# Linear attention staged one level ahead, operand splits shared with GpSimd at the half turn, and final rows reordered in a hybrid mixer and ConvFFN layer

## The chip, the cores and the metric

The kernel runs on one core of a Trainium2 chip. The metric is the device time of one execution in microseconds (us). Three runs of the kernel before gave 2209.49, 2205.0 and 2207.99 us, median 2207.99. The trace comes from one further execution of 2208.4 us, whose profiled span is 2206.6 us. Below, times in a trace count from the start of that span.

## What is computed

One decoder layer on x of 2048 positions by 1024 channels, all float32:

```
h = rms_norm(x, norm_mix_pre);  p = h @ w_in          # u, v_a, q, k, v_b, g_out, lr
out_a = u * (tril(w_s) @ layer_norm(v_a) + b_s)       # chunks of 128, 4 heads, after gelu
gk = log_sigmoid(lr @ w_gk + b_gk) / 16
out_b = rms_norm(gla(q, k, v_b, gk)) * silu(g_out)    # gated linear attention, 4 heads
x = x + rms_norm(concat(out_a, out_b) @ w_out, norm_mix_post)
up = causal_dwconv(rms_norm(x, norm_ffn_pre) @ w_up)  # 3 taps, 2 x 2816 channels
ff = (gelu(up[:, :2816]) * up[:, 2816:]) @ w_down
x = x + rms_norm(ff, norm_ffn_post)
```

## The kernel before

Every large product is made from float32r operands. An operand is split into a high part, which ScalarE casts (`A.copy(out=hi, in_=raw)`), and a low part, raw minus high, which `split_lo` (L77) gives to VectorE or to GpSimd. Three TensorE products, high by high, high by low and low by high, accumulate in PSUM, so nothing can be multiplied before both engines have split it.

The work has three phases. **Mixing** goes through four batches of 512 positions (`mix_in`). A batch makes q and k, then weaves two generators: `main`, which runs the gated linear attention of its two halves (`gla_half`), and `side`, which makes the other projections (`token_steps`: one weight chunk and its 24 products between two yields) and the output projection of the batch before (`mix_out`, tiles mx0a and mx1a). `weave` adds a ratio for each step of `main` and runs one step of `side` whenever the sum reaches one. `gla_half` first makes the decayed keys (kd, transposed to kps) and the diagonal (qk, dps). Then it goes through seven levels of distance s = 64 to 1 (`LEVELS`): VectorE forms two differences of the cumulated gates (e), ScalarE exponentiates, VectorE and GpSimd multiply into qup and klow, TensorE makes the scores (tile lv), and VectorE copies them by a mask into attn. Products with v (tiles o, s), a norm, and a transpose (tile ot, `finish`) follow. Here a scheduler orders each engine's queue by priority, which follows the order in which the code was written.

The last `mix_out` and the first operands of the next phase form the **seam**: seven combinations of the normalised x are loaded from DRAM (tiles ta) and split, and 22 up-projection units start.

**Up** makes both halves of the positions (1024 each) in 22 units of a seven-product fast matrix multiplication (`prod`, L725; products in the order 0, 5, 6, 4, 1, 3, 2, each of 12 matmuls). At the turn from the first half (units u00 to u021) to the second (u10 to u121) all seven operands (tiles tb) are loaded and split anew by `op_split` (L652 to L657). **Down** does the same for w_down in steps of half, product and group (`dsteps`; matmuls on L1077), while `plan` (L1097) hangs the final norm and the store of finished rows on certain steps: `fin_load` fetches x, `fin_scale` squares a row and takes the root, `fin_row` scales, adds x and stores. From the first up unit to the end, `in_order` (L615) fixes each engine's queue to the order of the code. All loads and stores of these phases are issued by SP, one after the other; an issue waits until its tile is free.

The FFN code runs through `op_split(acts[4])`, `op_split(acts[1])`, `op_split(acts[3])` and `op_split(acts[2])` in the first unit of the second half (`new`, from L934), all with the low parts on VectorE.

Of the kernel before, what the change touches and what calls it, by code (L numbers as in the profile page):

```python
# [37 lines left out]
def layer_kernel(ctx, tc, x, xT, w_ch, w_gl, w_tk, w_o, w_up, w_dn, w_gk, wsT, cols, conv, rows, sgub,  # L38
# [73 lines left out]
    def token_steps(srcs, kper, n, hh, hl, name, done):  # L112
        nk = kper * len(srcs)
        ps = [bank(f"{name}a{t}", acc=True) for t in range(TT)]
        for i, src in enumerate(srcs):
# [12 lines left out]
            yield last.ins  # L128

# [14 lines left out]
    def mix_phase(mp, late):  # L144
# [57 lines left out]
        def mix_in(b, prev):  # L202
# [215 lines left out]
        return mix_out(NB - 1, *prev)  # L418

    def gla_half(b, hb, cum, qT, kT, vb, sg, ohb, olb, state, attn, klow, qup, lvl_sb, sel_sb, w1, pend):  # L420
# [16 lines left out]
        kps = bank(f"{n}kps")  # L437
        for c in range(2):
            for ht in range(2):
                o = (c * 2 + ht) * P  # L440
                PE.transpose(out=kps[:, o:o + P], in_=kd[:, ht, c * P:(c + 1) * P], identity=ident)
        kdec = w1.tile([P, 512], F32, tag="kdec", name=f"{n}kdec", bufs=1)
        A.copy(out=kdec, in_=kps)
# [3 lines left out]
        dps = bank(f"{n}dps")  # L447
        for c in range(2):
            for ht in range(2):
                o = c * 4 + ht * 2  # L450
                PE.matmul(dps[:, o:o + 2], lhsT=qk[:, ht, c * P:(c + 1) * P], rhs=sel_sb,
                          start=True, stop=True)
        dg = w1.tile([P, 8], F32, tag="dg", name=f"{n}dg")
        V.tensor_copy(out=dg, in_=dps[:, 0:8])
        yield

        for li, s in enumerate(LEVELS):
            if li == 4 and pend:
                pend.pop()()
                yield  # L460
            g = 256 // (2 * s)
            gc = P // (2 * s)
# [12 lines left out]
            for par in range(2):  # L475
# [6 lines left out]
                            in1=ev[:, :, :, 0, :], op=ALU.mult)  # L482
            mk = lvl_sb[:, li * 64:(li + 1) * 64].rearrange("p (g s) -> p g s", s=s)
            ps = bank(f"{n}lv{s}")
            for c in range(2):
                for ht in range(2):
                    o = (c * 2 + ht) * P
                    PE.matmul(ps[:, o:o + P], lhsT=kl[:, ht, c * P:(c + 1) * P],
                              rhs=qu[:, ht, :, c * 64:(c + 1) * 64], start=True, stop=True)
            av = attn.rearrange("p c h (g two s) -> p (c h) g two s", two=2, s=s)  # L490
            V.copy_predicated(out=av[:, :, :, 1, :], mask=mk.unsqueeze(1).to_broadcast([P, 8, gc, s]),
                              data=ps.rearrange("p (x g s) -> p x g s", x=8, s=s))
# [3 lines left out]
        for c in range(2):  # L496
            t = hb * 2 + c
            ops = bank(f"{n}o{c}")
            for ht in range(2):
                PE.matmul(ops[:, ht * 256:(ht + 1) * 256], lhsT=eb[:, ht, c * P:(c + 1) * P],  # L500
                          rhs=state[:, ht, :], start=True, stop=False)
                for par in range(2):
                    h = ht * 2 + par
                    hs = slice(h * P, (h + 1) * P)
                    PE.matmul(ops[:, hs], lhsT=attn[:, c, h, :], rhs=vb[t][:, hs],
                              start=False, stop=(par == 1))
            sps = bank(f"{n}s{c}")
            for h in range(NH):
                r = slice((h % 2) * 64, (h % 2) * 64 + 64)
                o = c * 256 + h * 64  # L510
                PE.matmul(sps[r, (h // 2) * P:(h // 2 + 1) * P], lhsT=kdec[:, o:o + 64],
# [115 lines left out]
    def ffn_phase(fp, mix_rest, late):  # L627
# [142 lines left out]
        class Side:  # L770
# [3 lines left out]
            def scale(self):  # L774
                pass
# [446 lines left out]
```

## Time and profile before

| | |
|---|---|
| median of three runs | 2207.99 us |
| profiled execution: time, span | 2208.4 us, 2206.6 us |
| TensorE busy | 2102.8 us (95%), 9904 matmuls |
| VectorE, ScalarE, GpSimd busy | 1570.1, 963.7, 710.3 us |
| DRAM traffic | 345.65 MB, 157 GB/s over the span |

Busy time is the union of an engine's instructions. The clock column of the stretches below is the share of TensorE's full 2.4 GHz that was granted: 1.00 is 2.4 GHz, 0.50 is 1.2 GHz. In the wait view, "A <- B: t, n, m" says that A waited for B, t us in all, n times, at most m. In a timeline, the bracket at a row's end is the idle time of the engine before it and what ended it.

### The profile page before, as it was taken

Reading aid. Unit: us, or ns where it says so; the run is one execution under the profiler, and the core shown is the slowest. Engines: PE = TensorE matmul, PEld = TensorE weight load, DVE = VectorE, ACT = ScalarE, POOL = GpSimd, SP = SyncE. Lnnn points to the kernel's source line nnn. Section 1 sums busy time; section 2 is a strip of 40 time slices with the busy share of each in tenths; the row PEclk is TensorE's granted clock in tenths of the full one; section 3 lists DMA queues with packets and bytes.
Section 4 is the critical chain, followed back from the end, with each engine's and each line's share of the span. In section 5 each row is a group of like instructions: output and inputs, shape, how many; then the busy total and the mean of one; then the engine's idle time right before and its main releaser. Section 6 shows DMA issues by size and latency. Waiting matters only on the chain.

```text
span 2206.6 us, 27110 instructions
## 1 busy us (share of the span) xinstructions
PE 2102.8 (95%) x9904; PEld 1737.2 (79%) x9904; DVE 1570.1 (71%) x2039; ACT 963.7 (44%) x1536; POOL 710.3 (32%) x481
## 2 busy tenths in 40 slices
PE   8998999999999889999999997999999999999997
PEld 7787877787788767788888876877787778888876
DVE  6776757666766465788878879999999952344366
ACT  5444435444545545444455544334333333332342
POOL 3322232232312224555545544555555300000000
PEclk9999999999999999999999998999999999999999
DMA  8422245225423626455445463434444544344465
GB/s 280 136 69 72 75 152 169 74 77 169 156 87 103 217 92 221 178 183 183 147 145 185 149 228 110 158 133 163 162 153 157 201 148 151 129 155 154 146 252 224
DMA packets 139366, 338.80 MB, mean 154 GB/s; under 512 B 13008, under 2 KB 42080, under 8 KB 139232
## 3 DMA queue, kind: packets, MB, share of 16 engines
q1 hardware_dynamic: 134336, 328.57, 44.0%
q10 hardware_dynamic: 4896, 8.50, 1.1%
q8 instruction: 78, 1.28, 0.2%
q14 instruction: 56, 0.46, 0.1%
HBM read 245.26 MB, written 100.40 MB: 157 GB/s over the span
## 4 chain that ended last, share of the span: by engine, by line
PE 39%; DVE 18%; issue 4%; DMA 3%; ACT 2%; POOL 1%; SPq 0%; DVEq 0%; POOLq 0%; ACTq 0%
PE d0C L1077 3%; PE d1A L1077 3%; PE d1C L1077 3%; PE d0A L1077 3%; PE d0D L1077 2%; PE d1D L1077 1%; PE d1B L1077 1%; PE d0B L1077 1%; DVE ds L580 1%; DVE dw L579 1%; DVE dw L581 1%; DMA dw<-in_w_dn 1%; DVE ds L578 1%; PE u015G L725 0%; PE u017G L725 0%
## 5 line engine op out<-in xcount | busy, mean ns | idle before, releaser
L1064 POOL TENSOR_TENSOR o010r<-o010r,mhalf 128x4 f32<-128x4 f32 x1 | 1.0, 1007 | 357.1 <-DVE o010r L1063 357.1
L77 DVE TENSOR_TENSOR tal<-tal,tah 128x1024 fp32r<-128x1024 f32 x14 | 24.7, 1811 | 10.8 <-ACT tah L657 10.8
L77 DVE TENSOR_TENSOR tbl<-tbl,tbh 128x1024 fp32r<-128x1024 f32 x14 | 18.7, 1390 | 8.8 <-ACT tbh L657 8.8
L1077 PE MATMUL d0D<-d2wl,d02th 128*128 128x512 f32 x44 | 18.0, 408 | 3.8 <-DVE d2wl L77 3.8
L1077 PE MATMUL d0A<-d0wh,d00th 128*128 128x512 f32 x44 | 18.5, 420 | 2.8 <-DVE u121y L752 2.8
L77 DVE TENSOR_TENSOR d11tl<-d11tl,d11th 128x1024 fp32r<-128x1024 f32 (+1 forms) x6 | 6.6, 1134 | 20.3 <-ACT d11th L657 20.3
L77 DVE TENSOR_TENSOR d05tl<-d05tl,d05th 128x1024 fp32r<-128x1024 f32 (+1 forms) x6 | 6.6, 1133 | 19.7 <-ACT d05th L657 19.7
L1045 DVE TENSOR_TENSOR r<-d0C,du 128x512 f32<-128x512 f32 x8 | 5.2, 686 | 21.7 <-PE d0C L1077 21.7
L77 DVE TENSOR_TENSOR d01tl<-d01tl,d01th 128x1024 fp32r<-128x1024 f32 (+1 forms) x6 | 6.6, 1134 | 18.0 <-ACT d01th L657 18.0
L1077 PE MATMUL d0A<-d0wl,d00th 128*128 128x512 f32 x44 | 18.3, 417 | 0.0
L1077 PE MATMUL d0A<-d0wh,d00tl 128*128 128x512 f32 x44 | 18.1, 412 | 0.0
L77 DVE TENSOR_TENSOR d10tl<-d10tl,d10th 128x1024 fp32r<-128x1024 f32 (+1 forms) x6 | 6.6, 1135 | 16.2 <-ACT d10th L657 16.2
L477 POOL TENSOR_TENSOR qup<-b3q,b3h1e 64x256 f32<-64x256 f32 x7 | 6.0, 855 | 36.9 <-issue 15.0
L581 DVE TENSOR_TENSOR dw<-dw,ds 128x512 f32<-128x512 f32 x11 | 17.4, 1580 | 0.4
L580 DVE TENSOR_TENSOR ds<-dw,dw 128x512 f32<-128x512 f32 x11 | 17.4, 1579 | 0.4
L579 DVE TENSOR_TENSOR dw<-dw 128x512 f32<-128x512 f32 x11 | 17.4, 1578 | 0.4
L1077 PE MATMUL d0D<-d2wh,d02tl 128*128 128x512 f32 x44 | 17.6, 400 | 0.0
L1077 PE MATMUL d0D<-d2wh,d02th 128*128 128x512 f32 x44 | 17.6, 400 | 0.0
L1064 POOL TENSOR_TENSOR o110r<-o110r,mhalf 128x4 f32<-128x4 f32 x1 | 4.3, 4251 | 41.3 <-DVE o110r L1063 41.3
L1077 PE MATMUL d0A<-d1wl,d01th 128*128 128x512 f32 x44 | 17.1, 389 | 0.0
L1077 PE MATMUL d1B<-d5wl,d15th 128*128 128x512 f32 x44 | 17.1, 389 | 0.0
L1077 PE MATMUL d1D<-d2wl,d12th 128*128 128x512 f32 x44 | 17.1, 389 | 0.0
(4592 smaller groups left out, 8460.9 us busy)
## 6 DMA issues: line engine op xcount, KB each, us to landing
dw<-in_w_dn SPq DMA_DIRECT2D x22, 512.0 KB, 5.2
out<-r SPq DMA_DIRECT2D x16, 512.0 KB, 5.7
tal<-act SPq DMA_DIRECT2D x14, 512.0 KB, 6.6
tbl<-act SPq DMA_DIRECT2D x14, 512.0 KB, 6.4
wdn<-in_w_dn SPq DMA_DIRECT2D x6, 1024.0 KB, 7.4
wdn<-dw SPq DMA_DIRECT2D x22, 256.0 KB, 2.3
wdn<-ds SPq DMA_DIRECT2D x22, 256.0 KB, 3.1
d00tl<-ffs SPq DMA_DIRECT2D x5, 512.0 KB, 8.4
```

The lines of the kernel that those rows point to most:

```text
L77: eng.tensor_tensor(out=lo, in0=full, in1=hi.bitcast(F32), op=ALU.subtract)
L477: (G if par else V).tensor_tensor(out=qu[r, :, par, :].rearrange("p a (g s) -> p a g s", s=s), in0=view(q)[r, :, :, 1, :], in1=ev[r, :, :, ...
L578: eng.tensor_tensor(out=t3, in0=b22, in1=b12, op=ALU.subtract)
L579: eng.tensor_tensor(out=b12, in0=b12, in1=b11, op=ALU.subtract)
L580: eng.tensor_tensor(out=t2, in0=b22, in1=b12, op=ALU.subtract)
L581: eng.tensor_tensor(out=t4, in0=b21, in1=t2, op=ALU.subtract)
L1045: return V.tensor_tensor(out=row(half, o[0], t)[:, o[1] * T:(o[1] + 1) * T], in0=ps, in1=u, op=ALU.add)
L1064: G.tensor_tensor(out=rr[:, sl], in0=rr[:, sl], in1=mhalf[:, sl], op=ALU.pow)
L1077: ins = PE.matmul(ps, lhsT=lhs, rhs=wop[w][:, i], start=start and k == 0, stop=stop and k == 2, skip_group_check=more)
```

## The change

Four edits go together.

1. **Attention.** The e, exponent and product work of a level moves into `decays(li)`, which is written one level ahead of the scores of the level before; `scores`, the transposes and the products with v are pinned by `issue_after(newest_pe())` behind the last TensorE instruction written so far. In each chunk the state products (s) come ahead of the output products (o). Two more yields stand ahead of the last `finish` of a batch, and the weaving ratio goes from 0.85 to 0.8.
2. **Seam.** The first step of the last `mix_out` is written while the mixing pools are still open. The first unit's weights are split after the fourth operand of the seam instead of the second (the order of operands is 0, 5, 6, 4, 1, 3).
3. **Turn.** `op_split` takes an engine. Operand 4 is split one unit earlier, with its low parts on GpSimd; operand 3 goes to GpSimd; operand 1 comes behind the copy `copy_u2`.
4. **Final rows.** The x rows of the first finished quarter go into idle low-weight tiles and are all loaded at step last-7. The squares of the first 512 columns of the last four rows are summed two steps before the last (`part_scale`); at the end each row squares only its other 512 columns, the row before is finished while its own scale is made, and the last quarter's rows are scaled, added and stored in two halves.

```diff
+    def newest_pe():
+        return next(i for i in reversed(nc.cur_bb.bb.instructions) if i.engine == ET.PE)
...
                     yield from gla_half(b, hb, cum, qT, kT, vb, sg, ohb, olb, state, attn[hb], klow, qup,
                                         lvl_sb, sel_sb, w1, pend)
+                yield
+                yield
                 pend.pop()()
...
-            weave(main(), side(), (0.85, 0.85) if prev is not None else (0.62, 0.5))
+            weave(main(), side(), (0.8, 0.8) if prev is not None else (0.62, 0.5))
...
-        return mix_out(NB - 1, *prev)
+        rest = mix_out(NB - 1, *prev)
+        next(rest)
+        return rest
...
+        ready = decays(0)
+        yield
+        with tc.issue_after(newest_pe()):
...
+        for li in range(len(LEVELS)):
+            if li == 4 and pend:
+                pend.pop()()
+                yield
+            now = ready
+            if li + 1 < len(LEVELS):
+                ready = decays(li + 1)
+            scores(li, *now)
             yield
...
-        def op_split(op):
+        def op_split(op, eng=V):
...
-                split_lo(V, lo[:, sl], raw[:, sl], hi[:, sl])
+                split_lo(eng, lo[:, sl], raw[:, sl], hi[:, sl])
...
-        next(mix_rest)
...
-            if m == 5:
+            if m == 4:
                 prep = Prep("u00", first, raw4("u00s23"), raw4("u00s14"))
...
-            if new:
-                op_split(acts[4])
             product(0, None if end else pa)
...
-            if new:
-                op_split(acts[1])
...
                 copy_u2 = A.copy(out=f.u2, in_=pa)
+            if new:
+                op_split(acts[1])
             if nxt:
                 nxt.sums()
                 nxt.split(0)
+            if new:
+                op_split(acts[3], G)
...
-            if new:
-                op_split(acts[3])
...
                 op_split(pre[6])
+                op_split(pre[4], G)
...
-        plan = {last - 6: [lambda: loads(0, 1, 0, 1), lambda: scale(0, 1)],
-                last - 5: [lambda: finish(0, 1, 0, 1), lambda: loads(0, 1, 2, 3)],
-                last - 4: [lambda: finish(0, 1, 2, 3), lambda: loads(1, 1, 0, 1, 2, 3)],
+        plan = {last - 7: [lambda: loads(0, 1, 0, 1, 2, 3)],
+                last - 6: [lambda: scale(0, 1)],
+                last - 5: [lambda: finish(0, 1, 0, 1)],
+                last - 4: [lambda: finish(0, 1, 2, 3)],
...
             done = evac(m, half, t)
-            fin_row(half, 0, t, fin_scale(half, 0, [t]))
+            A.activation(out=junk[:, :T], in_=row(1, 0, t)[:, T:], func=AF.Square, accum_out=tail[:, t:t + 1])
+            if t:
+                fin_row(half, 0, t - 1, rt[:, t - 1:t], 2)
+            V.tensor_scalar(out=rt[:, t:t + 1], in0=tail[:, t:t + 1], scalar1=1.0 / D, scalar2=part[:, t:t + 1],
+                            op0=ALU.mult, op1=ALU.add)
+            G.tensor_tensor(out=rt[:, t:t + 1], in0=rt[:, t:t + 1], in1=mhalf[:, :1], op=ALU.pow)
+        fin_row(half, 0, TT - 1, rt[:, TT - 1:TT], 2)
```

The built program's queues show what moved. TensorE's queue at the end of the second half of batch 2, from the last level's scores (lv) to the first output products with attn (o<-b2vb,attn); vaa are projections. Before:

```order
L488 MATMUL b2h1lv_4465<-qup_206,klow_210 128x128 x4
L500 MATMUL b2h1o_4471<-state,b2h1eb 128x256
L123 MATMUL b2vaa_4580<-hb2vaw_4585,b2hi_3260 128x512
L124 MATMUL b2vaa_4580<-lb2vaw_4586,b2hi_3260 128x512
L125 MATMUL b2vaa_4580<-hb2vaw_4585,b2lo_3261 128x512
L123 MATMUL b2vaa_4580<-hb2vaw_4585,b2hi_3264 128x512
L124 MATMUL b2vaa_4580<-lb2vaw_4586,b2hi_3264 128x512
L511 MATMUL b2h1s_4478<-b2vb_3256,b2h1kdec 64x128 x4
```

Now:

```order
L481 MATMUL b2h1lv_4461<-qup_206,klow_210 128x128 x4
L524 MATMUL b2h1s_4468<-b2vb_3256,b2h1kdec 64x128 x4
L527 MATMUL b2h1o_4467<-state,b2h1eb 128x256
L532 MATMUL b2h1o_4467<-b2vb_3256,attn_204 128x128 x2
L527 MATMUL b2h1o_4467<-state,b2h1eb 128x256
L532 MATMUL b2h1o_4467<-b2vb_3256,attn_204 128x128 x2
```

Before, 14 projections lay between the last scores and the first o<-attn (the rows that follow those shown are nine more of them); now none does. Ahead of these scores stand 10 projections instead of 6, and ahead of the batch's last transposes 34 in one piece instead of 28. The place of kps and dps in the first half, 13 projections behind q and k and one more between the two, is the same in both.

SP's queue at the seam, where b3mx0w and b3mx1w are the weight chunks of the last output projection, u0r the raw weights of the first up unit, and tal the operands. Before:

```order
L86 DMA rb3u_6716<-in_w_ch 128x1024
L86 DMA rb3mx0w_6785<-in_w_o 128x1024
L86 DMA rb3mx0w_6831<-in_w_o 128x1024
L662 DMA u0rg<-in_w_up 128x1024
L86 DMA rb3mx0w_6869<-in_w_o 128x1024
L663 DMA u0rv<-in_w_up 128x1024
L86 DMA rb3mx0w_6941<-in_w_o 128x1024
L650 DMA tal_6824<-act_89 128x1024 x2
```

Now:

```order
L86 DMA rb3u_6716<-in_w_ch 128x1024
L86 DMA rb3mx0w_6764<-in_w_o 128x1024
L86 DMA rb3mx0w_6831<-in_w_o 128x1024
L86 DMA rb3mx0w_6869<-in_w_o 128x1024
L684 DMA u0rg<-in_w_up 128x1024
L685 DMA u0rv<-in_w_up 128x1024
L86 DMA rb3mx0w_6907<-in_w_o 128x1024
L86 DMA rb3mx1w_6965<-in_w_o 128x1024
L672 DMA tal_6824<-act_89 128x1024 x2
```

The first chunk (6785, now 6764) takes a tile of the mixing pool, and u0rv no longer stands behind the third chunk.

VectorE's queue at the turn, from the last split of the first half's last unit to the sums of the second half's first unit. Before:

```order
L77 TENSOR_TENSOR tbl_10687<-tbl_10687,tbh_10686 128x1024 x2
L77 TENSOR_TENSOR tbl_10710<-tbl_10710,tbh_10709 128x1024 x2
L897 TENSOR_TENSOR u021G<-u021G,u021u_10635 128x512
L749 SCALAR_TENSOR_TENSOR u021yv<-u021V,cv,u021yv 128x1023
L749 SCALAR_TENSOR_TENSOR u021yv<-u021V,cv,u021yv 128x1022
L77 TENSOR_TENSOR tbl_10731<-tbl_10731,tbh_10730 128x1024 x2
```

Now:

```order
L77 TENSOR_TENSOR tbl_10687<-tbl_10687,tbh_10686 128x1024 x2
L918 TENSOR_TENSOR u021G<-u021G,u021u_10635 128x512
L770 SCALAR_TENSOR_TENSOR u021yv<-u021V,cv,u021yv 128x1023
L770 SCALAR_TENSOR_TENSOR u021yv<-u021V,cv,u021yv 128x1022
L77 TENSOR_TENSOR tbl_10731<-tbl_10731,tbh_10730 128x1024 x2
```

Operand 4's pair (10710) has left VectorE here, and so has operand 3's pair behind the sums; operand 1's (10731) and, further on, operand 2's stay.

## Rows read from the trace of the kernel before

**Rows 1.** The page: TensorE's busy share in the 40 slices.

```profile
PE   8998999999999889999999997999999999999997
```

**Rows 2.** Stretches: mixing, seam, up, down, tail (us, engines' busy us, clock, DMA).

```profile
0.00:819.80 819.80, 769.72 (x4104) 646.87 (x4104) 542.16 (x925) 394.14 (x684) 215.96 (x158) 0.97 0.39 128
819.80:878.10 58.30, 49.25 (x193) 38.91 (x194) 34.97 (x23) 32.67 (x50) 25.26 (x11) 0.91 0.65 226
2193.10:2206.60 13.50, 0.02 (x1) 0.00 (x0) 5.93 (x7) 1.78 (x4) 1.08 (x2) 0.64 0.27 108
```

**Rows 3.** TensorE's waits in mixing.

```profile
PE b2h1ot L546 <- DVE b2h1os L537: 3.2, 2, 2.5
...
PE h2t L605 <- ACT h2x L590: 3.1, 1, 3.1
...
PE b2h1lv L488 <- DVE x1rm L557: 2.6, 1, 2.6
```

**Rows 4.** Stretches of batch 2: the wait for the last level, and what follows.

```profile
531.88:534.46 2.58, 0.00 (x1) 0.03 (x1) 2.55 (x5) 1.01 (x2) 1.60 (x2) 1.00 1.05 361
534.70:538.10 3.40, 3.40 (x13) 3.03 (x13) 2.33 (x3) 0.00 (x0) 1.01 (x1) 0.50 0.86 330
```

**Rows 5.** Timelines of VectorE and GpSimd around that wait.

```profile
530.23 2.63 DVE L477 TENSOR_TENSOR qup<-b2q,b2h1e 64x256 f32<-64x256 f32 x1
...
530.19 2.39 POOL L77 TENSOR_TENSOR lb2vaw<-rb2vaw,hb2vaw 128x1024 fp32r<-128x1024 f32 x1 [6.98 <-ACT hb2vaw L89]
```

**Rows 6.** TensorE's waits at and behind the seam, and two stretches of the seam.

```profile
PE b3mx0a L123 <- ACT hb3mx0w L89: 4.1, 1, 4.1
...
PE b3mx1a L124 <- POOL lb3mx1w L77: 3.1, 1, 3.1
...
PE u00V L725 <- DVE u00u L966: 2.9, 1, 2.9
...
PE b3mx0a L124 <- POOL lb3mx0w L77: 1.7, 1, 1.7
...
824.83:831.65 6.82, 5.36 (x13) 4.20 (x14) 2.63 (x2) 0.62 (x1) 2.76 (x2) 0.50 0.72 262
...
859.20:877.80 18.60, 18.60 (x82) 15.15 (x81) 8.27 (x6) 10.05 (x15) 2.41 (x1) 1.00 0.43 172
```

**Rows 7.** TensorE's waits at the turn and the clock across the longer one.

```profile
PE u10V L725 <- DVE u10u L966: 10.9, 1, 10.9
...
PE u10G L725 <- ACT u10u L944: 3.6, 1, 3.6
...
1333.42:1347.05 13.63, 5.57 (x13) 4.44 (x14) 11.48 (x12) 4.95 (x7) 6.74 (x4) 0.50 0.11 39
```

**Rows 8.** VectorE's and GpSimd's timelines at the turn.

```profile
1315.64 4.63 DVE L77 TENSOR_TENSOR tbl<-tbl,tbh 128x1024 fp32r<-128x1024 f32 x4 [2.21 <-ACT tbh L657]
...
1329.73 3.42 DVE L77 TENSOR_TENSOR tbl<-tbl,tbh 128x1024 fp32r<-128x1024 f32 x2
...
1338.37 2.36 DVE L77 TENSOR_TENSOR tbl<-tbl,tbh 128x1024 fp32r<-128x1024 f32 x2 [2.12 <-ACT tbh L657]
...
1326.55 1.52 POOL L77 TENSOR_TENSOR u11w0l<-u1rg,u11w0h 128x512 fp32r<-128x512 f32 x1 [14.81 <-ACT halo L758]
```

**Rows 9.** The wait in down's product D, VectorE ahead of it, and the clock behind it.

```profile
PE d0D L1077 <- DVE d2wl L77: 3.8, 1, 3.8
...
2133.13 1.22 DVE L1071 TENSOR_TENSOR r<-r,o6x 128x1024 f32<-128x1024 f32 x1 [5.26 <-DMA o6x<-x]
...
2142.37:2145.78 3.41, 3.12 (x7) 2.48 (x8) 3.41 (x6) 2.27 (x4) 1.88 (x1) 0.50 1.02 414
```

**Rows 10.** The tail: last evacuation, square, scaling and addition of the last row.

```profile
2197.09 0.68 DVE L1045 TENSOR_TENSOR r<-d1D,du 128x512 f32<-128x512 f32 x1
2197.87 1.06 ACT L1060 ACTIVATE o103q<-r 128x1024 bf16<-128x1024 f32 x1 [4.14 <-DVE r L1045]
2201.25 1.22 DVE L1071 TENSOR_TENSOR r<-r,o11x 128x1024 f32<-128x1024 f32 x1
```

More of the change, by code (lines that the diff above doesn't have):

```diff
@@ L436, in gla_half, with decays @@
         V.tensor_tensor(out=kd, in0=kd, in1=k, op=ALU.mult)
[L437 to L443, printed above, removed]
         qk = w1.tile([P, 2, 256], F32, tag="lv", name=f"{n}qk", bufs=4)
         V.tensor_tensor(out=qk, in0=q, in1=k, op=ALU.mult)
[L447 to L460, printed above, removed]
+        def decays(li):
+            s = LEVELS[li]
             g = 256 // (2 * s)
-            gc = P // (2 * s)
             def view(ap):
@@ L487, in gla_half @@
                     o = (c * 2 + ht) * P
[L488 to L492, printed above, removed]
+                    PE.transpose(out=kps[:, o:o + P], in_=kd[:, ht, c * P:(c + 1) * P], identity=ident)
+            for c in range(2):
+                for ht in range(2):
+                    o = c * 4 + ht * 2
+                    PE.matmul(dps[:, o:o + 2], lhsT=qk[:, ht, c * P:(c + 1) * P], rhs=sel_sb,
+                              start=True, stop=True)
+        kdec = w1.tile([P, 512], F32, tag="kdec", name=f"{n}kdec", bufs=1)
+        A.copy(out=kdec, in_=kps)
+        dg = w1.tile([P, 8], F32, tag="dg", name=f"{n}dg")
+        V.tensor_copy(out=dg, in_=dps[:, 0:8])
+        for li in range(len(LEVELS)):
[6 more added lines that the diff above has]
+            scores(li, *now)
             yield
@@ L543, in finish @@
                 tp = bank(f"{n}ot{c}")
-                for h in range(NH):
-                    hs = slice(h * P, (h + 1) * P)
-                    PE.transpose(out=tp[:, hs], in_=os[c][:, hs], identity=ident)
+                with tc.issue_after(newest_pe()):
+                    for h in range(NH):
+                        hs = slice(h * P, (h + 1) * P)
+                        PE.transpose(out=tp[:, hs], in_=os[c][:, hs], identity=ident)
                 tsl = slice(t * P, (t + 1) * P)
@@ L1048, in ffn_phase @@
         fin = {}
+        junk = acc.tile([P, D], F32, tag="row", name="junk", bufs=14)
         def fin_load(half, r, t):
             tt = half * 8 + r * TT + t
[L1052 to L1065 removed]
@@ L1067, in fin_row @@
-        def fin_row(half, r, t, rr):
+            if half == 0 and r == 1:
+                xr = [big.tile([P, T], F32, tag="wlo", name=f"o{tt}x{k}", bufs=8) for k in range(2)]
+                for k in range(2):
+                    nc.sync.dma_start(out=xr[k], in_=x1_d[tt][:, k * T:(k + 1) * T])
+            else:
+                x_all = acc.tile([P, D], F32, tag="row", name=f"o{tt}x", bufs=14)
+                nc.sync.dma_start(out=x_all, in_=x1_d[tt])
+                xr = [x_all[:, :T], x_all[:, T:]]
@@ new lines, in fin_load, with fin_scale @@
+            fin[half, r, t] = xr
+        def fin_scale(half, r):
+            ss = com.tile([P, 4], F32, tag="fs", name=f"o{half}{r}s", bufs=4)
+            for t in range(TT):
+                A.activation(out=junk, in_=row(half, r, t), func=AF.Square, accum_out=ss[:, t:t + 1])
+            rs = com.tile([P, 4], F32, tag="fr", name=f"o{half}{r}r", bufs=4)
+            V.tensor_scalar(out=rs, in0=ss, scalar1=1.0 / D, scalar2=EPS, op0=ALU.mult, op1=ALU.add)
+            G.tensor_tensor(out=rs, in0=rs, in1=mhalf[:, :4], op=ALU.pow)
+            return rs
@@ L1084, in ffn_phase, with part_scale @@
         rr = {}
+        part = com.tile([P, 4], F32, tag="fs", name="part", bufs=4)
         def scale(half, r):
-            rr[half, r] = fin_scale(half, r, range(TT))
+            rr[half, r] = fin_scale(half, r)
+        def part_scale():
+            for t in range(TT):
+                A.activation(out=junk[:, :T], in_=row(1, 0, t)[:, :T], func=AF.Square,
+                             accum_out=part[:, t:t + 1])
+            V.tensor_scalar(out=part, in0=part, scalar1=1.0 / D, scalar2=EPS, op0=ALU.mult, op1=ALU.add)
         def loads(half, r, *ts):
@@ L1127, in ffn_phase @@
                     evac(m, half, t)
+        tail = com.tile([P, 4], F32, tag="fs", name="tail", bufs=4)
+        rt = com.tile([P, 4], F32, tag="fr", name="rt", bufs=4)
         for t in range(TT):
```

76 lines of the change are left out of this document (44 added, 32 removed).

## The prediction

> **What bounds the kernel now.** I read the page first. TensorE is busy 95% of the span, and its slices [rows 1] show 8s in mixing and at the seam, one 7 near the turn and one 7 at the very end. So nothing can be won by making another engine cheaper; what can be won is TensorE's idle time, and what follows it. Then I read the busy time by stretches [rows 2]: mixing leaves TensorE idle for 819.80 - 769.72 = 50.1 us, and the seam takes 58.30 us. Third, the wait view says for whom TensorE waits in each of these [rows 3, 6, 7, 9]. Last, I looked at short stretches behind the waits. There the clock column matters: after a late wait of some us the granted clock is 0.50, that is 1.2 GHz [rows 4, 6, 9], and work at half clock takes twice as long. A wait thus costs its own length and half of the half-clock stretch behind it. The prices below are made so.
>
> The sum is made against the profiled execution, 2208.4 us, which is 0.4 above the median of the three runs, 2207.99.
>
> **Attention, written one level ahead.** In batch 2, TensorE waits 2.6 us for the last level's scores, and 3.2 us for two transposes [rows 3]. What delays the last level is seen in the timelines [rows 5]: VectorE's product qup, 64x256, takes 2.63 us while GpSimd makes a 2.39 us subtraction that began 0.04 us before it. Once this product is made ahead of the previous level's scores, there is a whole level of time for such a delay. The 2.58 us wait is followed by 3.40 us at clock 0.50 [rows 4]; for the wait for the transposes, which is as long, I take the same. So a batch loses 2.6 + 3.2 in waits and 2 x 3.40 / 2 = 3.4 in clock, 9.2 us. Batch 1 has the same waits, with 2.2 in place of 2.6: 8.8 us. Together the most that can go there is 18.0 us. What the change takes away as cover: 14 projections stood between the last scores and the first product with attn, and now none does, so VectorE's masked copy of the last scores lies open between them. The transposes get 34 projections ahead instead of 28, and the scores 10 instead of 6. The transposes' wait then is better covered, the last scores' wait too, but a new short wait ahead of o appears once a half. The pins cost nothing by themselves: they set an order, add no instruction, and hold no buffer. The start of a first half keeps its place in TensorE's queue, so I gain nothing there. I take two thirds of 18.0, **-12 us**; the ends are 0, if the new wait takes all of it, and -20, if the rest of batch 0 and 3 also gains a little.
>
> **Seam.** By the undisturbed stretch a matmul takes 18.60 / 82 = 0.227 us [rows 6]. The seam's 192 matmuls need 43.6 us and take 58.30 [rows 2], 14.7 more. Waits for the first weight chunk are 4.1 and 1.7, for the second chunk 3.1 [rows 6], 8.9 in all; the other 5.8 is clock, as one stretch of 6.82 us at 0.50 shows. The first chunk is now loaded from a tile of the mixing pool, which is free before the last mixing matmuls, so 4.1 + 1.7 + 6.82 / 2 = 9.2 us should go. The second chunk waits for GpSimd, whose queue holds seven splits of the first unit's weights ahead; these now come two operands later. Of its 3.1 and the half clock behind it (5.8 - 3.4 = 2.4) I take under half, 2.3. Sum **-11.5 us**; ends -6 (only the first chunk's 5.8 of waits) and -13.5 (all but about 1). Late next is the weight load of unit u1, for which u00's product 3 waits 2.9 us [rows 6]: it starts with the same issue as before, relative to the seam's end, or slightly earlier, as u0rv no longer stands behind the third chunk on SP's queue. I leave this wait.
>
> **Turn.** TensorE waits 3.6 us for ScalarE's copy of product 0 and 10.9 us for VectorE's second sum, L966, ahead of product 3 [rows 7]; 13.63 us around the latter are at 0.50. VectorE's queue [rows 8] holds ahead of that sum two pairs of splits in 4.63 us (operands 6 and 4), then one of 3.42 (operand 3) and one of 2.36 (operand 2). Operand 4's half, 2.3 us, goes to GpSimd and one unit earlier, operand 3's 3.42 goes too. GpSimd has 14.81 us without work there [rows 8], and a 128x1024 subtraction takes it 2.39 us [rows 5], so 4.8 per operand fits; operand 4 may come about 1 us late for its product, as it can begin no earlier than its cast. The copy comes ahead of operand 1's cast now, so the 3.6 goes. But product 3 also waits for operand 2's split, which was itself 2.12 us late behind ScalarE's cast [rows 8]. VectorE's 5.7 us are therefore an upper end of what product 3 can move, and 2.6, if ScalarE's casts hold the chain, a lower one. I take the middle, 4, as nothing that ScalarE does gets less; the 3.6 that goes earlier then only lengthens the wait for product 3; of the half clock, which costs 5.57 / 2 = 2.8 us in that stretch, 1 us is won. **-5 us**, ends -1 and -8.
>
> **Final rows in down.** The last product D waits 3.8 us for its low weights d2wl, behind VectorE, which stood 5.26 us for a row of x [rows 9]; 3.41 us at 0.50 follow, worth 1.7. The loads now all stand at one step earlier than their use, in tiles that are idle, so both waits should go: 3.8 + 1.7 = 5.5; I take **-5.3**, ends -2 (d2wl still late by its own load) and -5.5.
>
> **Tail.** TensorE ends near 2193.1 [rows 2], yet VectorE evacuates the last row only at 2197.09, because it first finishes the row before; then follow a square of 1.06 us, the root, and scaling and addition, until 2202.47 [rows 10]. A row took VectorE's chain 4.14 + 1.06 = 5.2 us, from square to square [rows 10], because VectorE stood while square and root were made. Now it finishes the row before in that time: 0.68 to evacuate, about 1.25 to scale, 1.22 to add and little else, some 3.5 us. So the lag of 4.0 us doesn't build up, and the last evacuation can begin soon after 2193.1. After it one row is to be finished (2.5), then the root of the last (about 1.2) and its two halves (2.5), which ends near 2200.2. That is 2.3 earlier. The last store is half as long: of 4.1 us between VectorE's end and the span's end at most half goes. I take 0.7: **-3 us**, ends -1 and -4.
>
> The sum: 12 + 11.5 + 5 + 5.3 + 3 = 36.8, and 2208.4 - 36.8 = 2171.6, against the median 2171.2. I say **2171**. All upper ends together give 51, 2157; all lower ends 10, 2198.
>
> **Rivals.** *The next chain takes over* (0.16). The attention waits go, but the transposes h1t and h2t of a batch's start wait for loads and norms of x 3.1 us for h2t [rows 3], and u00 for its product 3, 2.9 us [rows 6]: TensorE arrives earlier and waits there longer. For it speaks that both waits stand already and the change touches neither; against it, that they are short. Then mixing gives 2 and the seam 6: 2208.4 - (2 + 6 + 5 + 5.3 + 3) = 2187.
>
> *GpSimd is too slow at the turn* (0.07). Its 128x1024 subtraction takes 2.39 us [rows 5], VectorE's 4.63 / 4 = 1.16 [rows 8], and with both at work a VectorE product stretched to 2.63. Then operand 3 is late and VectorE's remaining splits stretch by what they lost: turn 0, the rest as above, 2177. The Trainium skill's "GPSIMD Engine Reference", section "4.1 Engine selection", says the same against this edit: elementwise work belongs on VectorE, GpSimd being about twice as slow for two inputs. The trace agrees, with 2.39 against 1.16; it does not say whose queue is empty, and GpSimd's 14.81 idle us decide for me.
>
> *Slower: the pinned queue* (0.04). TensorE can no longer run projections past a late score. Where GpSimd blocks a level's products, the scores wait 2.5 us and the clock takes another 1.7, 4.2 for each. Without mixing's gain 24.8 us are left, so it is slower from 6 of the 56 levels on; with 14 it would be 2208.4 - 24.8 + 58.8 = 2242. Against it: each level now has a whole step of lead.
>
> *Nothing happens* (0.03). The named waits go, but each is replaced by one of like length for the same engine further on, as the change removes no multiplication and no split: 2208.
>
> **How the numbers follow.** Forecast 0.70, and the four rivals above. Ends that miss all together are unlikely, as five terms are independent: the range leaves out the corner cases and takes in 2187 and 2177, so 2158 to 2191. A measurement of this kernel tells 0.2%, 4.4 us, from no change. Faster by more than that: 0.70 + 0.16 + 0.07 = 0.93; within 0.03; slower 0.04.
>
> **What would show it.** Right: the waits for lv and ot of batches 1 and 2 below 1 us each and no half clock behind them; the seam under 48 us; no wait for b3mx0a of over 1; product 3 of u10 4 us earlier after the start of u10, and GpSimd busy where it was idle; d0D without a wait; VectorE's last addition within 8 us of TensorE's end. Wrong: a wait for o<-attn in most halves of over 1 us with half clock behind it, lv waits next to GpSimd's subtractions, longer waits for h1t, h2t or u00's product 3 that give the gain back.

## The result and the profile after

The changed kernel took 2183.65 us (median of four runs, 2178.79 to 2188.09), against 2206.99 us for the kernel before in the same comparison. The ratio is 0.9893 with a 95% interval of 0.9868 to 0.9918, so the change makes the kernel about 23 us faster. The prediction was 2171, with a range of 2158 to 2191 and a chance of 0.93 for faster. The sign is right and the time lies in the range, but 37 us were forecast and 23 came.

The time of the profiled execution of the changed kernel is 2185.53 us, its span 2183.7 us. Its page begins with the engines' busy time:

```profile
PE 2091.9 (96%) x9904; PEld 1729.6 (79%) x9904; DVE 1559.5 (71%) x2056; ACT 965.4 (44%) x1544; POOL 712.1 (33%) x485
```

TensorE runs the same 9904 matmuls and is busy 10.9 us less than before, as fewer of them run at half clock: the mean granted clock of the execution is 0.983, before it was 0.978. The stretches that answer to [rows 2], and unit u10 and the first group of down besides:

```profile
0.00:806.50 806.50, 762.81 (x4105) 642.09 (x4106) 533.00 (x925) 394.82 (x685) 215.83 (x159) 0.98 0.40 130
806.50:863.60 57.10, 49.87 (x198) 39.24 (x197) 33.18 (x23) 31.87 (x49) 21.41 (x10) 0.91 0.62 221
1296.30:1333.90 37.60, 22.38 (x86) 16.90 (x85) 31.51 (x26) 17.47 (x23) 23.51 (x12) 0.82 0.32 125
1746.80:1784.40 37.60, 32.19 (x133) 25.72 (x133) 22.07 (x27) 13.26 (x15) 0.00 (x0) 0.95 0.48 171
2173.50:2183.70 10.20, 0.04 (x1) 0.00 (x0) 6.32 (x10) 0.72 (x2) 0.54 (x1) 0.68 0.31 116
```

Columns are as in [rows 2]. The same two stretches of the kernel before, u10 and the first group of down:

```profile
1310.70:1349.70 39.00, 24.23 (x86) 18.63 (x85) 33.40 (x30) 17.45 (x23) 13.48 (x8) 0.78 0.33 125
1762.50:1798.50 36.00, 33.15 (x134) 26.69 (x132) 22.03 (x27) 13.26 (x15) 0.00 (x0) 0.91 0.49 178
```

From this the change is taken apart. Mixing lost 13.3 us (819.8 to 806.5). The seam, counted from the last gate product to the last product of the output projection, lost 1.2 (58.3 to 57.1). Unit u10 lost 1.4. Down gained 1.6 at its start and lost 5.5 in its last product, which took 89.9 us instead of 95.4. The tail behind TensorE lost 3.3. Together that is 23.1; the two spans differ by 22.9.

TensorE's waits, in the same view as [rows 3, 6, 7, 9]:

```profile
PE u10V L746 <- DVE u10u L985: 13.8, 1, 13.8
...
PE b3mx0a L123 <- ACT hb3mx0w L89: 4.8, 1, 4.8
PE u00V L746 <- DVE u00u L985: 3.9, 1, 3.9
...
PE d0A L1109 <- DVE d0wl L77: 2.6, 1, 2.6
PE b3mx1a L124 <- POOL lb3mx1w L77: 2.4, 1, 2.4
PE b2h1ot L568 <- DVE b2h1os L558: 2.3, 2, 1.9
...
PE b2h1lv L481 <- DVE klow L468: 1.1, 1, 1.1
```

The waits for lv and ot of batches 1 and 2 are shorter, 6.8 us together instead of 11.2, and the one for d2wl is gone. But two waits that the forecast let go are still there: the seam still waits 4.8 us for a weight chunk, and product 3 of u10 now waits 13.8 us instead of 10.9. That one is longer because the 3.6 us wait ahead of it has gone, as forecast; product 3 starts 29.9 us into the unit, before it was 30.7. The wait for u00's product 3, which the forecast left alone, grew from 2.9 to 3.9. The experiments ask why.

Where a run was taken once, its whole time says little (runs of one kernel spread over 9 us); the lengths of its stages are compared instead. These spread too: mixing ends between 801.5 and 808.6 us in the eight traces with the changed attention code, the seam takes 55.2 to 58.2 us in the ten with the changed seam, and u10 37.0 to 38.2 in the nine with the changed turn.

### The profile page after: what moved, and what is told of

The parts are those of the page before. It is cut to its first block, busy times and chain, and to the rows that moved or that the text cites. A ratio compares the mean times of both kernels' runs of the same rounds, so it can differ in the third digit from the quotient of the medians.

```text
span 2183.7 us, 27160 instructions
## 1 busy us (share of the span) xinstructions
PE 2091.9 (96%) x9904; PEld 1729.6 (79%) x9904; DVE 1559.5 (71%) x2056; ACT 965.4 (44%) x1544; POOL 712.1 (33%) x485
## 4 chain that ended last, share of the span: by engine, by line
PE 60%; DVE 23%; issue 6%; ACT 5%; DMA 4%; POOL 2%; SPq 0%; DVEq 0%; POOLq 0%; ACTq 0%
PE d0C L1109 3%; PE d0D L1109 3%; PE d1A L1109 3%; PE d1C L1109 3%; PE d0A L1109 2%; PE d1D L1109 2%; PE d1B L1109 1%; PE d0B L1109 1%; DVE klow L468 1%; DVE ds L602 1%; DVE dw L601 1%; DVE dw L603 1%; DVE attn L484 1%; PE u01G L746 1%; PE u015G L746 1%
## 5 line engine op out<-in xcount | busy, mean ns | idle before, releaser
L77 DVE TENSOR_TENSOR tbl<-tbl,tbh 128x1024 fp32r<-128x1024 f32 x10 | 13.1, 1353 | 9.0 <-ACT tbh L679 9.0
L679 ACT CAST tah<-tal 128x1024 fp32r<-128x1024 f32 x14 | 14.6, 1047 | 8.1 <-DMA tal<-act 8.1
L1109 PE MATMUL d1B<-d5wh,d15th 128*128 128x512 f32 x44 | 17.1, 389 | 0.0
L1109 PE MATMUL d0C<-d3wl,d03th 128*128 128x512 f32 x44 | 17.1, 389 | 0.0
L1109 PE MATMUL d1A<-d1wh,d11tl 128*128 128x512 f32 x44 | 17.1, 389 | 0.0
L1109 PE MATMUL d1C<-d6wh,d16tl 128*128 128x512 f32 x44 | 17.1, 389 | 0.0
L1109 PE MATMUL d1D<-d4wh,d14tl 128*128 128x512 f32 x44 | 17.1, 389 | 0.0
L1109 PE MATMUL d1A<-d0wh,d10th 128*128 128x512 f32 x44 | 17.1, 389 | 0.0
L1109 PE MATMUL d0A<-d1wh,d01tl 128*128 128x512 f32 x44 | 17.1, 389 | 0.0
```

The lines of the kernel that those rows point to most:

```text
L77: eng.tensor_tensor(out=lo, in0=full, in1=hi.bitcast(F32), op=ALU.subtract)
L679: A.copy(out=hi[:, sl], in_=raw[:, sl])
L1109: ins = PE.matmul(ps, lhsT=lhs, rhs=wop[w][:, i], start=start and k == 0, stop=stop and k == 2, skip_group_check=more)
```

## Experiments

### Each part undone alone

Four kernels, each the changed kernel with one of its four parts as before (the diff of the section on the change, reversed for that part).

**Attention.** 

> The changed kernel with the attention part alone as before. Theory A (each part is worth what its own stage shows): mixing is 9 to 14 us longer than in the changed kernel, the other stages keep their lengths within 1 us; time near 2195. Rival P (the terms of the prediction): 12 us longer, 2196. Rival C (the gain in mixing was a matter of where the half-clock stretches fell, not of the edit): mixing differs by under 5 us, 2188 or less.

Measured: 2195.48 us. Mixing ends at 818.4 instead of 806.5, 11.9 us later, and the waits are those of before:

```profile
PE b2h1ot L551 <- DVE b2h1os L542: 3.2, 2, 2.5
PE b2h1lv L493 <- DVE x1rm L562: 2.4, 1, 2.4
```

So the part is worth about 12 us, as A and P say, and C falls.

**Seam.** 

> The changed kernel with the seam part alone as before. Theory A (the edit only moves the uncovered load from the first weight chunk to the second): from the end of the last gate product to the start of unit u01 0 to 3 us longer, time 2184 to 2187, and the wait for the first chunk's cast is back at 4 us while the second chunk's is gone. Rival P (the term of the prediction): 11.5 us longer, near 2195.

Measured: 2182.46 us. The stretch from the last gate product to the last output projection takes 58.7 us, of which the changed kernel's trace saves 1.6:

```profile
803.20:861.90 58.70, 50.28 (x194) 39.48 (x194) 34.56 (x23) 32.86 (x50) 25.20 (x11) 0.88 0.65 224
...
PE b3mx0a L123 <- ACT hb3mx0w L89: 4.0, 1, 4.0
```

The wait for the first chunk is back, and the 4.8 us for the second are gone, as theory A says. Against the 55.2 to 58.2 us of the ten traces with the part, it is worth 0.5 to 3.5 us in the seam, so P, which had 11.5, falls. About 1 us of that is lost again: u00's product 3 waits 2.9 us here and before, and 3.9 to 4.0 in those ten. Mixing ended 3.3 us earlier in this run than in the changed kernel's; that this comes from the edit is not shown.

**Turn.** 

> The changed kernel with the turn part alone as before, all low parts on VectorE. Theory A (what VectorE is spared it loses again to GpSimd's subtraction): unit u10 takes 38.9 us instead of 37.6, time 2184 to 2187. Rival P: 5 us longer, near 2189. In both VectorE's sums for the next unit (L698 to L700) take about 0.7 us each again instead of 2.8 for two of them.

Measured: 2186.39 us, u10 38.6 us, 1.0 more than in the changed kernel's trace and 0.4 above the longest of the nine with the part.

```profile
PE u10V L746 <- DVE u10u L987: 11.0, 1, 11.0
```

Product 1 waits 3.5 us again, and product 3 starts 30.7 us into the unit; in each of the nine it is 29.9. VectorE's sums L699 and L700 take 0.68 us each. A holds, and P, which had 5 us, falls.

**Final rows.** 

> The changed kernel with the final rows alone as before. Theory A: the wait for d2wl of 3.8 us is back, down's last products take 5.5 us longer and the end after TensorE's last product is 13.5 us instead of 10.2; time near 2192. Rival P (8.3 us): 2192 as well. Rival C (the wait at the start of down, 2.6 us for d0wl in the changed kernel, is made by this part): that wait goes and the time is near 2190.

Measured: 2194.26 us. The wait is back, down's last product takes 97.1 us, and 14.1 us follow TensorE's last matmul:

```profile
PE d0D L1097 <- DVE d2wl L77: 4.0, 1, 4.0
```

That is 7.2 + 3.9 = 11.1 us, more than the 8.3 forecast; behind the wait the granted clock is 0.50 for 6.8 us here (2125.8 to 2132.6), and was for 3.41 us before [rows 9]. The start of down takes 36.0 us in this run, which looks like C; but it takes 36.0 in the seam run and 37.6 in the turn run too, both with the new final rows. So the new rows alone do not make the longer one (see the last section). Six of the twelve traces with them have it, neither of the two with the old rows; that leaves C open.

### What in the attention part carries its 12 us

The part has three things in it: the lead of one level, the pins (with s ahead of o), and the two yields with the ratio of 0.8. First without the lead:

```diff
-        ready = decays(0)
         yield
...
-            now = ready
-            if li + 1 < len(LEVELS):
-                ready = decays(li + 1)
-            scores(li, *now)
+            scores(li, *decays(li))
```

> The changed kernel with every pin, but a level's exponents and products written right before its scores, not one level ahead. Theory A (the lead is what took the level waits away, and a pinned queue without it is worse than the queue of before): waits for lv over 2 us come back in all batches, mixing 10 us or more longer, time above 2193. Rival B (the pins and the order of s ahead of o carry the gain): mixing within 4 us of the changed kernel.

Measured: 2186.20 us, and mixing ends at 807.7, among the eight traces with the lead. The wait for the last level is as long as with it:

```profile
PE b2h1lv L481 <- DVE x1rm L575: 1.1, 1, 1.1
```

Theory A, which was the prediction's own, falls: no gain of the lead is seen. It is not taken away quite alone here, as 13 projections instead of 10 now stand ahead of the last scores. Then without the pins:

```diff
-            with tc.issue_after(newest_pe()):
+            with ExitStack():
```

(at all four places). 

> The changed kernel without any pin behind the newest TensorE instruction; the lead of one level, s ahead of o, the yields and the ratio stay. Theory A (the pins carry mixing's gain, as the lead alone does not): from the start to the last gate product 815 us or more instead of 806.5, time above 2191. Rival B (the pins do nothing): 804 to 809 us.

Measured: 2188.15 us, mixing ends at 809.5. A falls again. B, "the pins do nothing", said 804 to 809; 809.5 is just outside, and 0.9 above the longest of the eight traces with pins, so up to 3 us may be theirs. Then only the yields and the ratio taken back:

```diff
-                yield
-                yield
                 pend.pop()()
                 yield
-            weave(main(), side(), (0.8, 0.8) if prev is not None else (0.62, 0.5))
+            weave(main(), side(), (0.85, 0.85) if prev is not None else (0.62, 0.5))
```

> The changed kernel with the ratio at 0.85 and without the two yields ahead of a batch's last transposes. Theory A (the pins carry mixing's gain): up to the last gate product within 3 us of the changed kernel's 806.5, the wait for ot grows from 1.9 to at most 2.7. Rival B (the ratio and the yields carry it): 812 us or more.

Measured: 2197.18 us, mixing ends at 818.2, with lead and pins in place. The waits are back in full:

```profile
PE b1h1ot L566 <- DVE b1h1os L556: 3.2, 2, 2.5
...
PE b2h1lv L479 <- DVE klow L466: 2.5, 1, 2.5
```

So theory B of this run holds, and the reverse must work: the attention code of before, with the ratio and the yields alone.

> The changed kernel with the attention code of before (no lead, no pins, o ahead of s), but with the ratio at 0.8 and the two yields: in TensorE's queue 13 projections then stand ahead of a batch's last scores, where before had 6, the changed kernel 10 and the run with the old ratio 3. Theory A (the ratio and the yields alone carry mixing's gain, by the projections that they leave for these places): up to the last gate product 804 to 809 us, as the changed kernel's 806.5, the wait for the last level at most 1.2 us, time 2179 to 2188. Rival B (the gain needs the lead and the pins as well): 812 us or more, time above 2190.

Measured: 2183.96 us, mixing ends at 806.9:

```profile
0.00:806.90 806.90, 761.46 (x4105) 641.18 (x4106) 529.99 (x925) 394.45 (x685) 213.80 (x159) 0.98 0.40 130
...
PE b2h1ot L553 <- DVE b2h1os L544: 2.5, 2, 1.8
...
PE b2h1lv L495 <- DVE x1rm L564: 1.0, 1, 1.0
```

Theory A holds: the ratio and the two yields carry the part, as far as these traces can tell. The three traces with the old ratio and no yields end mixing at 818.2 to 819.8 us, the eleven with the new ones at 801.5 to 809.5. How they do it stands in TensorE's queue. In batch 1, the projections between the last but one level's scores and the last level's, and those ahead of the last transposes:

| kernel | ahead of the last scores | wait for lv | ahead of the last ot | longest wait for ot | mixing ends |
|---|---|---|---|---|---|
| before | 6 | 2.2 | 28 | 2.5 | 819.8 |
| lead and pins alone | 3 | 2.5 | 28 | 2.5 | 818.2 |
| changed kernel | 10 | 1.1 | 34 | 1.9 | 806.5 |
| ratio and yields alone | 13 | 1.2 | 32 | 1.9 | 806.9 |

A smaller ratio makes `side` fall behind `main`, so projections are left for the end of the batch, where the waits are. The last scores are not ready much sooner: from the last but one scores to the last 3.65 us pass in batch 1 before, 3.40 in the changed kernel and 4.20 in the last run. But of these, projections fill 1.4, 2.3 and 3.0 us. With the lead the stretch is somewhat shorter (3.40 us, and 3.17 with lead and pins alone) than without it (3.65 and 4.20). Whether the ratio or the yields do more was not tried.

### Why the seam still waits

SP's queue in the changed kernel, and TensorE's row behind the wait:

```profile
812.13 0.80 SPq L86 DMA_DIRECT2D rb3mx0w<-in_w_o  x2
...
816.82 1.22 PE L123 MATMUL b3mx0a<-hb3mx0w,b3oh 128*128 128x512 f32 x2 [4.75 <-ACT hb3mx0w L89]
```

The first chunk is indeed loaded early, at 783.58, into a tile of the mixing pool. But the second chunk's tile (the second of the projection's first half; what the prediction calls the second chunk is the first of its second half, b3mx1w) lies in the pool that is opened over the closed one's memory, and its load starts at 812.13, right after the first chunk's last product (812.07). In the built program this load waits for that very matmul, because the new pool covers the tile of the first chunk's high parts. The 24 products moved ahead and took the place where the wait begins along with them. To test it, the weight pool stays open:

```diff
-        wpool.append(mp.enter_context(tc.tile_pool(name="wm", bufs=3)))
+        wpool.append(lates.enter_context(tc.tile_pool(name="wm", bufs=2, side="right")))
+        third.append(mp.enter_context(tc.tile_pool(name="wt", bufs=1)))
...
+            place = third[0] if third and wcount[0] % 3 == 2 else pool
-            hi = pool.tile([P, 1056], F32R, tag="whi", name=f"h{name}")
+            hi = place.tile([P, 1056], F32R, tag="whi", name=f"h{name}")
...
-    wpool[:] = [late.enter_context(tc.tile_pool(name="wl", bufs=2, side="right"))]
+    third.clear()
```

> The changed kernel, but the pool that holds a weight chunk's raw, high and low tiles stays open from mixing into the seam (two of the three high and low slots on the right side of the memory, the third one in mixing alone). Theory A (the second chunk's load waits for the closed pool's last reader, the first chunk's last product): the load is issued before mixing ends, the wait of 4.8 us for the second chunk's cast falls below 1 us, and the seam's 192 products with their waits take 48 to 52 us instead of 57.0; the wait for a low part of the second half's chunks, 2.4 us behind GpSimd's splits, stays or grows to 5. Rival B (the load itself, its queue or the cast is too slow): the wait stays above 3 us.

Measured: 2177.27 us. Its queue and its waits:

```profile
791.10 11.98 SPq L87 DMA_DIRECT2D rb3mx0w<-in_w_o  x2
...
PE b3mx1a L126 <- POOL lb3mx1w L77: 5.3, 1, 5.3
...
801.50:855.70 54.20, 48.77 (x201) 39.01 (x200) 33.67 (x23) 30.80 (x48) 22.32 (x10) 0.94 0.60 213
```

The second chunk's load is issued at 791.10, before mixing ends, and the four first chunks' 96 products run without a wait. Theory A's cause is shown. Its size is not: the seam takes 54.2 us, less than in each of the ten traces of above, but not 48 to 52, since the next wait in line, for a low part that stands behind GpSimd's splits of u00's weights, grew from 2.4 to 5.3 us.

### Why the turn gained so little

VectorE and GpSimd in unit u10 of the changed kernel:

```profile
1312.30 2.83 DVE L699 TENSOR_TENSOR u10s<-u1rg,u1rv 128x512 f32<-128x512 f32 x1
1315.05 2.82 DVE L700 TENSOR_TENSOR u10s<-u10s,u1rg 128x512 f32<-128x512 f32 x1
...
1323.10 2.36 DVE L77 TENSOR_TENSOR tbl<-tbl,tbh 128x1024 fp32r<-128x1024 f32 x2 [2.12 <-ACT tbh L679]
...
1311.79 5.53 POOL L77 TENSOR_TENSOR tbl<-tbl,tbh 128x1024 fp32r<-128x1024 f32 x2
...
1321.07 1.06 ACT L980 ACTIVATE u021y<-u021y 128x1024 f32<-128x1024 f32 x1 [1.98 <-DVE u021y L770]
```

While GpSimd subtracts operand 3 (5.53 us), two sums of VectorE take 2.83 and 2.82 us. Without that neighbour, each takes 0.68, as the next run shows. So VectorE gives back 4.3 us of the 5.7 it was spared. The filter taps behind the sums, the gelu (1321.07) behind the taps, operand 2's cast behind the gelu and its split behind the cast are all late by that. Operand 3 back on VectorE:

```diff
-                op_split(acts[3], G)
+                op_split(acts[3])
```

> The changed kernel, operand 3's low parts on VectorE again at the same place in the code. Theory A (GpSimd's subtraction takes VectorE's sums with it: 2.83 and 2.82 us instead of 0.7): these sums take 0.7 us again, VectorE pays about 2.4 to 3.4 us for the pair, so unit u10 takes 36 to 38 us, no more than the 37.6 with GpSimd. Rival B (the offload helped and only ScalarE's casts held product 3): u10 takes 39.5 or more.

Measured: u10 36.7 us; 2187.74 us for the whole.

```profile
1315.48 0.68 DVE L699 TENSOR_TENSOR u10s<-u1rg,u1rv 128x512 f32<-128x512 f32 x1
1316.08 0.68 DVE L700 TENSOR_TENSOR u10s<-u10s,u1rg 128x512 f32<-128x512 f32 x1
1316.68 3.42 DVE L77 TENSOR_TENSOR tbl<-tbl,tbh 128x1024 fp32r<-128x1024 f32 x2
```

Theory A holds: u10 is 0.9 us shorter with the split on VectorE, and product 3 starts 29.0 us into the unit instead of 29.9. Next, GpSimd keeps the split, but VectorE works on PSUM meanwhile:

```diff
-            if nxt:
+            if nxt and not new:
                 nxt.sums()
                 nxt.split(0)
...
-            if new:
-                op_split(acts[2])
             if not end:
                 add_u3 = V.tensor_tensor(out=u3, in0=pc, in1=f.u2, op=ALU.add)
+            if new:
+                op_split(acts[2])
+                nxt.sums()
+                for k in (0, 5, 6):
+                    nxt.split(k)
```

> The changed kernel; in the turn's unit VectorE does the sums on PSUM and the two filter taps of the unit before first, then operand 2's split, and only then the next unit's sums; operand 3 stays on GpSimd. Theory A (VectorE's queue order and the shared subtraction hold product 3): the wait for product 3 falls from 13.8 to under 4 us, u10 from 37.6 to between 24 and 30 us, time 2170 to 2177. Rival B (ScalarE's casts are the bound): the wait goes on to operand 2's product and u10 takes 33 us or more.

Measured: 2180.19 us, u10 32.6 us.

```profile
1311.63 2.60 DVE L770 SCALAR_TENSOR_TENSOR u021y<-u021G,cv,u021y 128x1023 f32<-128x1023 f32 x2
...
1310.67 5.00 POOL L77 TENSOR_TENSOR tbl<-tbl,tbh 128x1024 fp32r<-128x1024 f32 x2 [2.09 <-ACT tbh L679]
...
PE u10G L746 <- DVE u10V L998: 4.7, 1, 4.7
...
PE u10V L746 <- DVE u10u L983: 2.2, 1, 2.2
```

The wait for product 3 falls from 13.8 to 2.2 us, as A says; the taps, which read one operand from PSUM, take 1.3 us each beside GpSimd's subtraction. The Trainium skill's "SBUF — State Buffer", section "Who interferes with whom", says that a VectorE instruction with two SBUF inputs contends with a GpSimd instruction that reads SBUF, and one with at most one SBUF input, outside its two-port modes, does not. The trace agrees: 2.83 against 0.68 us for the sums, and for a pair of taps 2.60 us here against 2.59 in the turn run (at 1306.18), where GpSimd was idle. But u10 is longer than A's 24 to 30, and a new wait of 4.7 us stands ahead of product 2. It is not for ScalarE's casts, as rival B had it, but for VectorE's third sum (L998), which this order put behind the next unit's sums.

### A version that beats both

The third sum then goes ahead too, with operand 2 and the gelu behind it; the pool stays open; the low parts of u00's weights go to VectorE, and u01's weights are loaded before the operand that waits for the closed pools:

```diff
-                    prep.split(k)
+                    prep.split(k, V)
...
+        raws = load_up(1)
         run(mix_rest)
...
             side.turn(0)
+            if new:
+                product(4, pd, apart=(copy_u2,))
+                add_c22 = V.tensor_tensor(out=pb, in0=pd, in1=u3, op=ALU.add)
+                op_split(acts[2])
+                A.activation(out=prev.y, in_=prev.y, func=AF.Gelu_apprx_tanh)
+                nxt.sums()
+                for k in (0, 5, 6):
+                    nxt.split(k)
```

> The changed kernel with four edits: the weight pool stays open across the seam; the low parts of the first unit's weights at the seam on VectorE, not GpSimd; unit u01's weights loaded ahead of the operand that waits for the closed pools; in the turn's unit the three sums on PSUM and operand 2 come ahead of the next unit's sums. Theory A (these waits were queue order and a closed pool): no wait over 1.5 us for mixing's last weight chunks, u00's product 3 under 1.5 us, product 3 and product 2 of u10 together under 4 us; seam's 192 products in 45 to 49 us, u00 in 19 to 21 us instead of 23.8, u10 in 24 to 29 us instead of 37.6; time 2155 to 2165. Rival B (VectorE becomes the bound at the seam, and the next unit's weights at the turn): u00 over 23 us or u11 over 22 us, time above 2170.

Measured, as the median of five runs: 2171.46 us (2166.85 to 2172.05), ratio to before 0.9833, interval 0.9814 to 0.9852. That interval lies below the changed kernel's, 0.9868 to 0.9918, so this kernel beats both. Seam, u00, u10 and u11:

```profile
806.20:859.80 53.60, 49.75 (x201) 39.07 (x200) 30.92 (x30) 30.59 (x49) 7.37 (x3) 0.94 0.66 235
859.80:877.90 18.10, 17.96 (x78) 14.18 (x77) 9.73 (x12) 8.67 (x14) 10.28 (x8) 1.00 0.77 290
1286.80:1310.70 23.90, 20.35 (x86) 15.39 (x85) 19.86 (x19) 14.17 (x17) 12.94 (x6) 1.00 0.37 147
1310.70:1337.90 27.20, 21.46 (x86) 16.61 (x85) 26.31 (x29) 10.88 (x17) 20.16 (x13) 0.94 0.36 135
```

u10 falls from 37.6 to 23.9 us and u00 from 23.8 to 18.1, as A says or better. The time is above A's 2155 to 2165, and the seam's 53.6 above its 45 to 49, for two waits that took the place of the old ones:

```profile
PE u11V L750 <- DVE u11u L987: 4.7, 1, 4.7
PE b3mx1a L125 <- ACT b3mx0a L416: 3.6, 1, 3.6
...
838.79 0.58 ACT L415 COPY b3mo<-b3mx0a 128x512 f32<-128x512 f32 x1 [5.71 <-DMA mix<-b3mo]
```

One is rival B's: the next unit's sums are now late, and u11 takes 27.2 us where an undisturbed unit takes 19.1. At the turn, then, and in the time above 2170, B came true too. The other is new: with the weights in time, the second half of the projection waits for the first half's evacuation on ScalarE, which itself stands 5.71 us for a store. Of the four edits only the open pool was also tried alone.

## Why the prediction was right, and where it was wrong

- **The sum.** 36.8 us were forecast and 23.1 came, a gap of 13.7: the seam gave 10.3 less, the turn 3.6, down 1.4, while attention gave 1.3 more and the tail 0.3. The places were the right ones. Of the signs of being right three came (GpSimd busy at the turn, no wait of d0D, VectorE's end within 8 us of TensorE's) and the others did not: lv still waits 1.1 and ot 2.3 us in each of the two batches, the seam takes 57.1, b3mx0a waits 4.8, and product 3 of u10 starts 0.8 us earlier, not 4.
- **Attention, -12:** 13.3 measured, 11.9 when undone. The size is right by luck, and the step that made it is wrong: "Once this product is made ahead of the previous level's scores, there is a whole level of time for such a delay." No gain of the lead was seen. Nor did the waits for lv and ot go: they gave 4.4 of the 11.2 us that the 18.0 counts on. Most of the rest is the clock, as TensorE's time at half clock in mixing fell from 47.8 to 37.5 us and its busy time from 769.72 to 762.81. The prediction had the right count in its text, 34 projections instead of 28 and 10 instead of 6, and took it for a side effect. It also took lost cover into account, 14 projections ahead of the products with attn, and no wait came from it.
- **Seam, -11.5:** 1.2 measured, outside the term's own ends of 6 and 13.5. The step that failed is "so 4.1 + 1.7 + 6.82 / 2 = 9.2 us should go". A load that waits for a closed pool was seen to start late, but not asked what it waits for. Had it been, the second chunk would have been found to wait for the first chunk's products. For what it calls the second chunk it took 2.3: that wait (b3mx1a) fell from 3.1 to 2.4, and lies between 0.8 and 3.1 in the ten traces with the part.
- **Turn, -5:** 1.4 measured, 1.0 when undone. "Operand 4's half, 2.3 us, goes to GpSimd", and operand 3's 3.42 too, was priced as if GpSimd worked for nothing. Yet the 2.63 us product of [rows 5] had shown VectorE's price. This was the rival "GpSimd is too slow at the turn", given 0.07; product 3 started 29.9 us into the unit instead of 30.7, 0.8 us earlier, where the prediction's lower end was 2.6, a figure for which it shows no working. It is not GpSimd's slowness but what it does to VectorE's sums.
- **Down, -5.3:** the last product lost 5.5, and d2wl's wait is gone. The 1.6 us at the start of down were not forecast; half of the traces with the new final rows do not have them, and whether the edit has a part in them stays open.
- **Tail, -3:** 3.3 measured. VectorE ends 7.1 us after TensorE (2173.54 to 2180.68), the forecast worked out to 7.1. The last rows:

```profile
2173.57 0.69 DVE L1065 TENSOR_TENSOR r<-d1D,du 128x512 f32<-128x512 f32 x1 [1.17 <-PE d1D L1109]
...
2179.99 0.69 DVE L1102 TENSOR_TENSOR r<-r,o11x 128x512 f32<-128x512 f32 x1
```

VectorE now waits for TensorE at the last row, where before it came 4.0 us late to it [rows 10].

The rival "next chain takes over" (2187) was the nearest in time, but mostly wrong in its places: the wait for h1t went from 2.1 to 2.3 us and that for h2t fell from 3.1 to 2.1, and mixing gave 13.3 us, not 2. It was right on u00's product 3, which now waits 3.9 us instead of 2.9.

## What to carry to other kernels

When loads are moved ahead over the closing of a pool, ask of each load which instruction last used its memory: the wait goes with the last reader, not with the first load. An offload to GpSimd is priced by what VectorE runs beside it, so put VectorE's work on PSUM there. And where a weaver fills gaps with independent matmuls, try its ratio first, by counting what stands ahead of each late wait in the queue; it gave here, as far as the traces tell, all that the rewrite of the inner loop gave.

## What the runs showed that was not expected

A wait of the same length may or may not be followed by half clock. Two waits for ot in the changed kernel, one in batch 1, one in batch 2, and what follows each:

```profile
333.70:335.60 1.90, 0.03 (x2) 0.05 (x1) 1.90 (x2) 0.50 (x1) 1.59 (x1) 1.00 0.32 127
335.60:342.40 6.80, 6.80 (x32) 5.57 (x33) 4.77 (x8) 3.22 (x5) 0.00 (x0) 1.00 0.77 248
542.10:544.00 1.90, 0.03 (x1) 0.02 (x1) 1.90 (x2) 0.52 (x1) 1.61 (x1) 1.00 0.42 168
545.51:548.92 3.41, 3.41 (x10) 2.63 (x9) 2.33 (x3) 1.46 (x3) 0.00 (x0) 0.50 0.77 312
```

So batch 1, from the last gate product of batch 0 to its own, became 8.1 us shorter and batch 2 2.1, though the waits for lv and ot shrank by 2.0 and 2.4 us: time at half clock fell from 17.1 to 3.4 us in the one and from 13.7 to 10.2 in the other. In the eight traces with the changed attention code batch 1 takes 206.7 to 210.6 us, in the three with the old ratio 215.0 to 215.3.

At the start of down the half clock can even hide a wait. Before, TensorE ran at 0.50 early in the stage, and no wait for the low weights d0wl is seen; the changed kernel stood 2.6 us for them, and its half clock came behind:

```profile
1770.32:1777.14 6.82, 6.13 (x15) 4.82 (x16) 5.57 (x9) 6.05 (x7) 0.00 (x0) 0.50 0.44 163
...
1764.07:1767.48 3.41, 3.41 (x9) 2.66 (x9) 3.41 (x4) 0.00 (x0) 0.00 (x0) 0.50 0.85 232
```

Where there is a wait for d0wl, it ends 17.0 us into down. The stage takes 36.0 us in the eight traces with half clock ahead of that place and 37.6 in the six with half clock behind it. A forecast that prices every wait with its half clock is therefore good to some us and no better; why one wait is followed by it and another is not stays open.
